# A transformer layer on one core: the first norm's scale vector spread by TensorE instead of by a broadcast load, with a renewed order table

## The chip, the cores and the metric

One core of a Trainium2 chip runs the whole layer as one program. The metric is the device time of one execution in microseconds; the time before is the median of three executions, 1282.27 us (1280.33 to 1286.3).

## The reference

One layer over x, 1024 tokens by 1024 channels, batch 1, all in f32:

```python
hn = rms_norm(x, g_mix)            # x * rsqrt(mean(x*x) + 1e-6) * g_mix
proj = hn @ w_in                   # split into 17 pieces for four token mixers
# a: compressed, selected and windowed attention with gates   b: short convolution
# c: stick-breaking attention                                 d: dilated attention
groups = rms_norm(concat(o_a, o_b, o_c, o_d), g_out)
x = x + groups @ w_out
h2 = rms_norm(x, g_ffn)
return x + (silu(h2 @ w_gate) * (h2 @ w_up)) @ w_down
```

The change touches how `g_mix`, 1024 numbers, gets to the first norm, and the order of nearly all instructions.

## The kernel before

Every f32 product is made as three TensorE products: each operand is split into a high part (a rounded copy by ACT) and a low part (the rest, by DVE or POOL), and `mm3` (L241 to L244) adds high x high, high x low and low x high into PSUM.

**The start.** TensorE gets 32 transposes of the identity matrix that nobody reads (L73 to L76, `WARM`). SP, which issues nearly all DMAs in order, loads the first 128 rows of x (512 KB, L209), the scale vector `gbc` (L212: the same 4 KB row of `g_mix` to each of the 128 partitions, 512 KB written), the next rows of x, and two tiles of weights `wr` (536 KB each, L215, the w_in columns of `wA2`). Then come small constants (L218, L429), the other x tiles, and in L132 the pieces of a further weight, `wa`.

For each of the eight x tiles `normed_rows` (L171 to L186) does: ACT squares the tile with a sum (L175), DVE scales the sum (L179), POOL raises it to the power -0.5 (L180), DVE multiplies x by that number and by `gbc` into `xn` (L185; the first tile in two halves). `norm_transpose` (L188 to L200) then has TensorE transpose `xn` in two groups of four blocks (L196) into PSUM tiles `Tp` (two buffers), from which ACT writes the high part `XH` (L199) and DVE the low part `XL` (L200). The weights in `wr` are split by ACT into `whi` (L108) and by POOL into `wlo` (L109). With those, `proj_tok` (from L255) multiplies a token tile with `wA2`, 24 matmuls of 268 columns for each tile.

**After the start** come the other projections, the attention mixers, the output product, the FFN in Strassen-like products (`winograd`, `level2`), and the last product with `w_down`.

**What sets the order.** The program is traced once. `make_plan` (L2008) plays a list scheduler over it, `_planned` (L1852): on each engine, of the instructions that are ready in its own model of durations, it takes the one with the smallest due time. `DUE` (L1359) holds the due times as differences, one for each of the 9668 instructions ahead of the last stage (`PINNED_UNTIL`); the running sum is the due time. `fix_order` (L2018) then ties each engine's instructions to the planned order. So an engine waits at an instruction of the plan even where a later one could run. The 1465 instructions of the last stage, the product with `w_down`, have no due times.

```python
        while later[e] and later[e][0][0] <= t:
            r, i = heappop(later[e])
            heappush(now[e], (due[i], i))
        i = heappop(now[e])[1]
```

Of the kernel before, what the change touches and what calls it, by code (L numbers as in the profile page):

```python
# [9 lines left out]
F32 = mybir.dt.float32  # L10
# [7 lines left out]
D = 1024  # L18
NT = T // 128
KT = D // 128  # L20
# [7 lines left out]
WARM = 32  # L28
# [24 lines left out]
def hybrid(ctx, tc, pools, x, gmix, wa1, wa2, wkv, wcv, wd, wc, bgate, gcols, pe, w1, w2,  # L53
           convw, gout, wout, gffn, wgate, wup, wdown, c_wa, c_wsp, c_wd, c_wc, c_ind, out):
    nc = tc.nc
    cst = pools(ctx, "cst")
# [12 lines left out]
    ident = identr.bitcast(F32)  # L69
# [3 lines left out]
    if WARM:  # L73
        wm = pat_.tile([128, 512], F32, tag="O", bufs=NB["O"], name="Op")
        for _ in range(WARM):
            nc.tensor.transpose(wm[:, :128], ident, ident)  # L76
    gcol = cst.tile([128, 6], F32, name="gcol")
# [129 lines left out]
    for t in range(NT):  # L207
        xt = smq.tile([128, T], F32, tag="QK", bufs=QKB, name="xt")
        nc.sync.dma_start(xt, x[t * 128:(t + 1) * 128, :])  # L209
        xts.append(xt)  # L210
        if t == 0:
            nc.sync.dma_start(gbc, bass.AP(tensor=gmix.tensor, offset=gmix.offset, ap=[[0, 128], [1, D]]))  # L212
        if t < 2:
            wr = sm.tile([128, 2 * T], F32, tag="V", bufs=2, name="wr")
            nc.sync.dma_start(wr[:, :4 * 268].rearrange("p (k n) -> p k n", n=268), wa2[:, 4 * t:4 * t + 4, :])  # L215
            wraws.append(wr)
# [240 lines left out]
    for z, src in ((0, KK), (1, VV)):  # L457
# [22 lines left out]
        tp = Ttile()  # L480
# [17 lines left out]
        if z == 0:  # L498
# [7 lines left out]
            tp = Ttile()  # L506
# [1615 lines left out]
```

## Time and profile before

| | us |
|---|---|
| median of three runs (lowest, highest) | 1282.27 (1280.33, 1286.3) |
| the profiled execution's own time | 1282.15 |
| its span in the trace | 1280.4 |
| TensorE (PE) busy | 1261.8, 99% of the span |
| weight loads (PEld) busy | 1087.2, 85% |
| VectorE (DVE) busy | 1021.0, 80% |
| ScalarE (ACT) and GpSimd (POOL) busy | 696.6 and 695.0, 54% each |

The profiled execution took 1282.15 us, 1.75 us more than its span, and lies 0.12 us below the median. An engine's busy time adds up its instructions; the remainder is idle time, which the trace puts down to what released the next instruction. All times inside the trace are counted from the start of the span.

### The profile page before, as it was taken

How to read it: one execution, taken by the hardware profiler on the slowest of the kernel's cores; microseconds unless marked ns; L12 is line 12 of the kernel's file. 1: busy time of each engine (PE TensorE's matmuls, PEld its weight loads, DVE VectorE, ACT ScalarE, POOL GpSimd, SP SyncE). 2: the span in 40 equal slices, each digit the busy share in tenths (PEclk: the TensorE clock that was granted, in tenths of full speed). 3: DMA queues.
4: the chain of work that ended last, by engine and by line, in shares of the span. 5: the costliest groups of instructions: out<-in, count | busy, mean ns of one | idle time of the engine just before them, and what ended most of it. 6: DMA issues, size and time to landing. Idle time of an engine off the chain costs nothing.

```text
span 1280.4 us, 20588 instructions
## 1 busy us (share of the span) xinstructions
PE 1261.8 (99%) x7161; PEld 1087.2 (85%) x7161; DVE 1021.0 (80%) x1843; ACT 696.6 (54%) x1383; POOL 695.0 (54%) x514
## 2 busy tenths in 40 slices
PE   8999999999999999999999999999999999999998
PEld 8888888888899898999878878888888888887887
DVE  6868888888889889844778888996888977699862
ACT  6567677768889778635653333332333335523540
POOL 6453362645557344336753556564665654665655
PEclk9999999999999999999999999999999999999999
DMA  6340030212211315544644464344324339852534
GB/s 240 110 135 1 9 108 9 75 36 54 55 38 41 91 59 173 165 132 128 221 152 138 164 204 167 124 148 147 134 100 141 120 131 336 308 181 66 148 101 155
DMA packets 91416, 161.45 MB, mean 126 GB/s; under 512 B 10224, under 2 KB 33264, under 8 KB 91312
## 3 DMA queue, kind: packets, MB, share of 16 engines
q1 hardware_dynamic: 90752, 158.31, 38.3%
q0 software_dynamic: 560, 1.84, 0.4%
q8 instruction: 56, 0.92, 0.3%
q14 instruction: 48, 0.39, 0.1%
HBM read 119.47 MB, written 36.44 MB: 122 GB/s over the span
## 4 chain that ended last, share of the span: by engine, by line
PE 91%; DVE 3%; DMA 2%; ACT 2%; issue 1%; POOL 1%; SPq 0%; DVEq 0%; POOLq 0%; ACTq 0%
PE PRp L242 12%; PE PRp L244 12%; PE PRp L243 12%; PE Tp L571 4%; PE PRp L1156 3%; PE PRp L1158 3%; PE PRp L1157 3%; PE SPp L525 2%; PE SPp L523 2%; PE Op L577 2%; PE Op L576 2%; PE Tp L1156 2%; PE Tp L1158 2%; PE Tp L1157 2%; PE SPp L1156 2%; PE SPp L1158 2%
## 5 line engine op out<-in xcount | busy, mean ns | idle before, releaser
L109 POOL TENSOR_TENSOR wlo<-raw,whi 128x512 fp32r<-128x512 f32 x94 | 128.4, 1373 | 93.5 <-ACT whi L108 64.8
L559 ACT ACTIVATE pth<-Tp 128x512 fp32r<-128x512 f32 (+2 forms) x172 | 89.4, 529 | 51.1 <-PE Tp L571 26.2
L560 DVE TENSOR_TENSOR ptl<-Tp,pth 128x512 fp32r<-128x512 f32 (+2 forms) x172 | 103.0, 605 | 16.1 <-ACT pth L559 14.5
L1227 DVE TENSOR_TENSOR fw<-sraw,fw 128x512 fp32r<-128x512 f32 x73 | 89.7, 1251 | 30.5 <-ACT fw L1226 27.7
L1145 POOL TENSOR_TENSOR fw<-fraw,fw 128x512 fp32r<-128x512 f32 x50 | 75.3, 1511 | 67.4 <-ACT fw L1144 63.4
L1227 POOL TENSOR_TENSOR hw<-bB,hw 128x512 fp32r<-128x512 f32 x55 | 82.0, 1507 | 48.5 <-ACT hw L1226 48.5
L571 PE MATMUL Tp<-ident,S 128*128 128x128 f32 x552 | 103.5, 274 | 0.6 <-DVE ptl L560 0.6
L242 PE MATMUL PRp<-XH,whi 128*128 128x512 f32 x224 | 90.6, 408 | 0.0
L244 PE MATMUL PRp<-XH,wlo 128*128 128x512 f32 x224 | 89.7, 405 | 0.0
L243 PE MATMUL PRp<-XL,whi 128*128 128x512 f32 x224 | 89.7, 406 | 0.0
L1144 ACT ACTIVATE fw<-fs 128x512 fp32r<-128x512 f32 x72 | 43.5, 628 | 84.9 <-DVE fs L1089 61.4
L654 POOL TENSOR_SCALAR S<-S,ll 128x640 f32<-128x640 f32 (+7 forms) x32 | 54.6, 1708 | 60.8 <-DVE ll L652 25.6
L108 ACT ACTIVATE whi<-raw 128x512 fp32r<-128x512 f32 x102 | 62.8, 620 | 36.6 <-PE PRp L243 21.2
L571 PEld LDWEIGHTS Tp<-ident,S 128*128 128x128 f32 x552 | 69.1, 140 | 8.8 <-DVE ptl L560 0.8
L1145 DVE TENSOR_TENSOR fw<-fs,fw 128x512 fp32r<-128x512 f32 x72 | 69.5, 985 | 3.5 <-ACT fw L1144 3.2
L804 POOL TENSOR_TENSOR S<-S,R 128x128 f32<-128x128 f32 (+7 forms) x32 | 47.7, 1491 | 42.0 <-DVE R L802 32.0
L243 PE MATMUL PRp<-wlo,MH 128*128 128x256 f32 (+1 forms) x248 | 68.7, 289 | 0.0
L242 PE MATMUL PRp<-whi,MH 128*128 128x256 f32 (+1 forms) x248 | 67.6, 291 | 0.6 <-DVE dkr L322 0.6
L244 PE MATMUL PRp<-whi,ML 128*128 128x256 f32 (+1 forms) x248 | 66.9, 288 | 0.4 <-DVE ML L831 0.4
L1226 ACT ACTIVATE hw<-bB 128x512 fp32r<-128x512 f32 x62 | 38.8, 627 | 48.3 <-PE Op L244 18.8
L1226 ACT ACTIVATE fw<-sraw 128x512 fp32r<-128x512 f32 x73 | 45.6, 625 | 28.1 <-DMA sraw<-hS 16.4
L649 ACT ACTIVATE S<-S,mm 128x640 f32<-128x640 f32 (+7 forms) x64 | 47.0, 734 | 17.9 <-DVE mm L550 15.8
(569 smaller groups left out, 4577.7 us busy)
## 6 DMA issues: line engine op xcount, KB each, us to landing
fraw<-in_wgate_dram SPq DMA_DIRECT2D x22, 512.0 KB, 4.2
fraw<-in_wup_dram SPq DMA_DIRECT2D x22, 512.0 KB, 4.3
bB<-in_wdown_dram SPq DMA_DIRECT2D x44, 256.0 KB, 5.1
sraw<-hS SPq DMA_DIRECT2D x44, 256.0 KB, 2.7
raw<-in_wout_dram SPq DMA_DIRECT2D x30, 256.0 KB, 2.9
hS<-s SPq DMA_DIRECT2D x30, 256.0 KB, 2.3
sraw<-hA SPq DMA_DIRECT2D x29, 256.0 KB, 4.0
xt<-in_x_dram SPq DMA_DIRECT2D x8, 512.0 KB, 7.4
```

What stands on the lines that cost most here:

```text
L109: (lo or nc.gpsimd).tensor_tensor(dst_lo, raw, f(dst_hi), op=OP.subtract)
L242: nc.tensor.matmul(ps, a[0], b[0], start=first, stop=False)
L243: nc.tensor.matmul(ps, a[0], b[1], start=False, stop=False)
L244: nc.tensor.matmul(ps, a[1], b[0], start=False, stop=last)
L559: nc.scalar.activation(ph[:, c], tp[:, :n], AF.Copy)
L560: nc.vector.tensor_tensor(pl[:, c], tp[:, :n], f(ph[:, c]), op=OP.subtract)
L571: nc.tensor.transpose(tp[:, i * 128:(i + 1) * 128], p, ident)
L1145: eng.tensor_tensor(wt[:, 1, :], a, f(wt[:, 0, :]), op=OP.subtract)
L1156: nc.tensor.matmul(ps, wt[:, 0, c], bh[:, k, :], start=k == 0, stop=False)
L1158: nc.tensor.matmul(ps, wt[:, 1, c], bh[:, k, :], start=False, stop=k == 3)
L1226: nc.scalar.activation(wt[:, 0, :], raw, AF.Copy)
L1227: eng.tensor_tensor(wt[:, 1, :], raw, f(wt[:, 0, :]), op=OP.subtract)
```

## The change

Three things. `g_mix` comes from the host as 8 columns of 128 and is loaded as that, 4 KB in pieces of 32 bytes for each partition (`gmc`). Eight TensorE transposes of a column repeated 128 times put it into two `Tp` tiles, every partition with the same row, and two DVE copies bring them to `gbc`. The warm-up transposes go from 32 to 20. And the `DUE` list is another one over its whole length (9666 entries), fitted to the new program.

```diff
-WARM = 32
+WARM = 20
...
         for _ in range(WARM):
             nc.tensor.transpose(wm[:, :128], ident, ident)
+    gmc = cst.tile([128, KT], F32, name="gmc")
+    nc.sync.dma_start(gmc, gmix)
...
         if t == 0:
-            nc.sync.dma_start(gbc, bass.AP(tensor=gmix.tensor, offset=gmix.offset, ap=[[0, 128], [1, D]]))
+            for j in range(2):
+                tp = Ttile()
+                for k in range(4):
+                    nc.tensor.transpose(tp[:, k * 128:(k + 1) * 128],
+                                        gmc[:, 4 * j + k:4 * j + k + 1].to_broadcast([128, 128]), ident)
+                nc.vector.tensor_copy(gbc[:, j * 512:(j + 1) * 512], tp)
...
 DUE = """
--37755 1210 -1715 1864 149 -14756 334 80 152 75 -251 117 106 28 150 49 116 89 66 141 46 40 143 102 107 12 67 74 -27
...
-    d["gmix"] = np.asarray(i["g_mix"])[0]
+    d["gmix"] = np.asarray(i["g_mix"])[0].reshape(8, 128).T
```

The running sums of the two lists for what stands at the start of SP and TensorE (a smaller one goes first among those that are ready):

| instruction | due before | due after |
|---|---|---|
| DMA `gbc` (512 KB) / `gmc` (4 KB) | -38254 | -29488 |
| DMA x tile 0 | -37893 | -29435 |
| DMA `wr`, first half | -37152 | -28452 |
| DMA `wa`, first piece (256 KB) | -36029 | -28237 |
| DMA `go` (4 KB) | -36860 | -27871 |
| DMA `wr`, second half | -37815 | -27812 |
| DMA `pet` (16 KB) | -34613 | -25747 |
| DMA x tile 1 | -37588 | -25173 |
| DMA x tile 5 | -36383 | -25067 |
| DMA x tile 2 | -37062 | -24551 |
| first five warm-up transposes | -51003 to -50362 | -42099 to -41823 |
| the other 27 / 15 warm-up transposes | -50613 to -48756 | -38185 to -37391 |
| eight transposes of `gmc` | none | -42495 to -38644 |

SP follows these sums at the start but for `wr`, whose tiles come behind x tile 1 before the change. In the attention part (100 to 550 us of the planner's own time) the sums before and after differ by some hundreds and are correlated by 0.9 and more in each 50 us. In the first 100 us and from 600 us on (the FFN) they differ by thousands and up, with a correlation below 0.9, in some 50 us of the FFN near zero.

## Rows read from the trace of the kernel before

**Rows 1.** The page's first part: busy us of each engine (share of the span), instructions.
```profile
PE 1261.8 (99%) x7161; PEld 1087.2 (85%) x7161; DVE 1021.0 (80%) x1843; ACT 696.6 (54%) x1383; POOL 695.0 (54%) x514
```

**Rows 2.** Windows: start:end, length, busy us (instructions) of PE..POOL, granted clock, DMA share, GB/s.
```profile
40.00:120.00 80.00, 77.15 (x542) 70.85 (x541) 59.97 (x166) 49.72 (x130) 38.21 (x33) 1.00 0.26 82
760.00:800.00 40.00, 38.38 (x190) 30.97 (x189) 34.28 (x50) 13.72 (x26) 25.32 (x18) 1.00 0.52 178
800.00:1060.00 260.00, 260.00 (x1240) 215.09 (x1239) 222.32 (x278) 90.26 (x163) 155.68 (x109) 1.00 0.39 132
1080.00:1120.00 40.00, 40.00 (x173) 32.21 (x172) 25.82 (x21) 23.38 (x42) 26.58 (x18) 1.00 0.91 316
```

**Rows 3.** Timeline: start, us, engine, line, what, xcount [idle before <- releaser]. Warm-ups, x0.
```profile
2.21 6.66 PE L76 MATMUL Op<-ident 128*128 128x128 f32 x32 [2.21 <-DVE ident L72]
...
4.44 1.06 ACT L175 ACTIVATE xn<-xt 128x1024 f32<-128x1024 f32 x1 [2.43 <-DMA xt<-in_x_dram]
...
5.62 0.15 DVE L179 TENSOR_SCALAR ssm<-ss 128x1 f32<-128x1 f32 x1 [3.46 <-ACT xn L175]
...
6.53 1.42 DVE L185 SCALAR_TENSOR_TENSOR xn<-xt,ss,gbc 128x512 f32<-128x512 f32 x2 [0.76 <-POOL ss L180]
...
8.71 1.04 PE L196 MATMUL Tp<-ident,xn 128*128 128x128 f32 x8
```

**Rows 4.** Timeline: x tile 1, the weight split, the first matmuls.
```profile
7.83 1.06 ACT L175 ACTIVATE xn<-xt 128x1024 f32<-128x1024 f32 x1 [2.24 <-DMA xt<-in_x_dram]
...
9.57 0.60 ACT L199 ACTIVATE XH<-Tp 128x512 fp32r<-128x512 f32 x1 [0.59 <-PE Tp L196]
9.83 1.29 DVE L185 SCALAR_TENSOR_TENSOR xn<-xt,ss,gbc 128x1024 f32<-128x1024 f32 x1 [0.67 <-POOL ss L180]
10.06 0.64 ACT L108 ACTIVATE whi<-wr 128x536 fp32r<-128x536 f32 x1
...
10.75 0.39 PE L242 MATMUL PRp<-whi,XH 128*128 128x268 f32 x1 [1.01 <-ACT whi L108]
10.78 2.82 POOL L109 TENSOR_TENSOR wlo<-wr,whi 128x536 fp32r<-128x536 f32 x2 [0.98 <-ACT whi L108]
11.04 1.28 DVE L200 TENSOR_TENSOR XL<-Tp,XH 128x512 fp32r<-128x512 f32 x2
...
11.78 0.65 PE L196 MATMUL Tp<-ident,xn 128*128 128x128 f32 x4 [0.63 <-DVE XL L200]
...
12.36 0.40 PE L243 MATMUL PRp<-wlo,XH 128*128 128x268 f32 x1
...
12.71 0.28 PE L242 MATMUL PRp<-whi,XH 128*128 128x268 f32 x1
...
12.84 0.28 PE L243 MATMUL PRp<-wlo,XH 128*128 128x268 f32 x1
```

**Rows 5.** Windows at the start (columns as in Rows 2).
```profile
0.00:4.44 4.44, 2.23 (x11) 2.23 (x12) 0.73 (x7) 1.29 (x2) 1.29 (x11) 1.00 0.55 172
0.00:7.83 7.83, 5.62 (x27) 5.62 (x28) 2.19 (x10) 2.44 (x4) 1.85 (x12) 1.00 0.73 248
...
7.00:8.00 1.00, 1.00 (x6) 1.00 (x5) 0.94 (x2) 0.17 (x1) 0.00 (x0) 1.00 0.99 385
8.00:9.00 1.00, 1.00 (x10) 1.00 (x9) 0.00 (x0) 0.98 (x2) 0.00 (x0) 1.00 1.02 412
```

**Rows 6.** Timeline of SP: the first issue.
```profile
0.73 0.39 SPq L209 DMA_DIRECT2D xt<-in_x_dram  x1
```

**Rows 7.** DMA issues: what, queue, count, KB each, median us from issue to landing.
```profile
go<-in_gout_dram SPq DMA_DIRECT2D x1, 4.0 KB, 8.4
zq<-cqh SPq DMA_DIRECT2D x16, 32.0 KB, 1.8
```

**Rows 8.** Window from the end of the last matmul (columns as in Rows 2).
```profile
1276.66:1280.40 3.74, 0.00 (x0) 0.00 (x0) 0.69 (x1) 0.00 (x0) 0.00 (x0) 1.00 0.37 140
```

**Rows 9.** A window of the last stage (columns as in Rows 2).
```profile
1175.00:1185.00 10.00, 8.44 (x29) 6.18 (x28) 10.00 (x9) 4.91 (x9) 8.31 (x5) 0.83 0.25 63
```

638 rows, old and new, of the table DUE are left out of this document.

## The prediction

> **What bounds the kernel now.** I read the busy times first: TensorE is busy for 1261.8 of the span's 1280.4 us [rows 1], so all its idle time is 18.6 us. Then wide windows, to see whether busy means full pace: in 1080 to 1120 us, 173 matmuls take 40.00 us, 0.231 us each, and from 800 to 1060 us TensorE does not idle at all [rows 2]. Then the timeline of the start, because that is what the change rebuilds.
>
> There the reader is to see this. TensorE runs 32 warm-up transposes from 2.21 us on, 6.66 us long. x tile 0 has landed by 4.44 us, its scale is there just before 6.53, and DVE makes `xn` in two halves of 0.71 us each; the first is ready at 7.24. Yet its transposes begin at 8.71, behind the last warm-up [rows 3]. Then TensorE idles for 1.01 us until `whi` is there (10.75) and for 0.63 us until a `Tp` buffer is free (11.78), and has continuous work from 12.36 on [rows 4]. Meanwhile the loads run at 385 to 412 GB/s [rows 5]. x tile 1 lands at 7.83, behind `gbc`.
>
> TensorE bounds the kernel, so a saving counts only where it takes idle time out of TensorE or lets its real work start sooner. At the start that is 1.64 us of idle time and what the warm-ups hold back.
>
> [...]
>
> **The warm-ups and the spread.** Removed: 12 transposes of the identity. Added: 8 of `gmc`. The 32 cost 6.66 us, 0.208 each, so 28 end at 2.21 + 28 x 0.208 = 8.03 instead of 8.7. By the due sums the eight stand behind the first few warm-ups, with 15 behind them. `gmc` is issued first, so x tile 0 goes one issue later, about 0.4 us [rows 6]; its first half of `xn` is then ready at 7.24 + 0.4 = 7.65, covered by the warm-ups. The two copies to `gbc` are new on DVE; the nearest row is `XL`, 0.64 us each [rows 4]. They fall where DVE idles, 3.46 us ahead of L179 [rows 3], and end by about 6, before the scale of tile 0 (6.4 + 0.4). So x0's transposes start at about 8.15 instead of 8.71: **0.55 us** sooner.
>
> When does `gmc` land? No row has a 4 KB load into empty queues. The nearest are 1.8 us for 32 KB in a quiet part and 8.4 us for the 4 KB of `go` behind 2 MB of loads [rows 7]. It is first, so I take 2 us: 0.73 + 2 = 2.7 us, after two or three warm-ups, no wait. At 8.4 it would be 9.1 us, and TensorE, whose order is fixed, would stand at the first transpose of `gmc` with 15 warm-ups and all of x0 queued behind it (the last rival).
>
> The pace: six transposes start in the us before 8.0 and ten in the next [rows 5], the same instruction at 0.208 us and then at about half of that. [...] Afterwards 28 transposes stand there, and I take the rise where it was. If it comes later, x0's eight transposes take 1.7 instead of about 0.9 us and the first matmuls double too: up to 1.3 us lost. If it comes earlier, next to nothing is gained.
>
> [...]
>
> **The load taken out, and the new order of loads.** There are 512 KB less to move, 1.3 us at 400 GB/s. But the due sums also put weights first: x0, `wr`, a piece of `wa`, `go`, `wr`, `pet`, and only then x1. When x1 landed, 7.83 x 248 = 1942 KB had moved, 400 KB more than the three loads up to it hold; for x0 it was 4.44 x 172 = 764 KB, 250 KB more [rows 5]. With 330 to 400 KB:
> - `wr`, first half: 1052 + 330 KB, moved at about 6.4 us. `whi` (0.64) can follow then instead of at 10.06, and two `wlo` (POOL, 1.41 each [rows 4]) by 10. The wait for `whi` goes.
> - x1: 2376 + 330 to 400 KB, moved at 9.7 to 9.9 instead of 7.83: **2 us later**.
>
> What is late next: from x0's transposes to its `XH` it is 9.57 - 8.71 = 0.86 us, and 0.60 for ACT, so the first matmul goes from 10.75 to about 8.15 + 1.51 = 9.66. x0's 24 matmuls at 0.125 (two starts, 12.71 and 12.84) take 3.0 us, until 12.7. x1 needs 11.12 - 7.83 = 3.29 us from landing to `xn` [rows 4], so it is there at 13.1. TensorE idles 0.4 us for it and 0.6 us for its `XH`, until 14.7. By then it has done 0.87 + 3.0 + 0.87 = 4.74 us of real work (a group of eight transposes counted as 0.87). Before, by 14.7, it had done 0.87 for x0, 0.56 (four transposes and one matmul) and 14.7 - 12.36 = 2.34: 3.77. **Ahead by 0.97 us**, which contains the 0.55. From there on both run without gaps, as an x tile comes every 1.3 us and feeds 3.9 us. Bounds: all idle time gone and the earlier start, 1.64 + 0.55 = 2.2 us gained; or x1 later still and the rise missed, 1 us lost.
>
> **The due times of the rest.** No row shows what a new order costs. Idle time left to win: 18.6 less 2.2 ahead of the first instruction, 1.6 at the start and 3.7 behind the last matmul [rows 8] is 11 us, of which 2.85 lie in 40 to 120 us and 1.6 in 760 to 800 [rows 2]. To lose: a stall such as the one at 1175 to 1185, where TensorE idles for 1.56 us and the granted clock falls to its lower level for a while, 0.83 as a mean of 10 us [rows 9]: 1.7 us more, 3.3 in all. (That stall lies in the last stage, which has no due times.) I take a gain of 0.9 us, a third of the 2.85, because the loads of the next projections' weights move ahead most there; the bounds are a gain of 7.8 us (third rival) and a loss of 6.6 (two such stalls).
>
> **Sum.** 1282.15 (the profiled execution, 0.12 below the median) - 0.97 - 0.9 = 1280.3 us. A measurement of this kernel can tell about 0.5%, 6.4 us, from no change: faster is below 1275.9, slower above 1288.7. So I forecast no change that can be told, a shade on the fast side: chance 0.56, with 1278 to 1283 as its own range.
>
> **Rivals.**
> - *The start is given back* (0.12). x1's 2 us of delay, or a later wait for an x tile, takes what the earlier weights bring. For it: x1 has the longest chain at the start. Against: x0 alone feeds 3 us. Time: 1282.2.
> - *The new order stalls TensorE in the FFN* (0.15), the case on the slow side. Place: 800 to 1060 us, where it never idles, so nothing can be won. Price: 1.6 us for a stall (as in 760 to 800, clock at 1.00), 3.3 with the clock's fall. One such stall decides against the gains, two with the fall give 1280.3 + 6.6 = 1286.9, three 1290.2. For it: the due sums there hardly resemble the old ones. Against: 260 us without one now.
> - *The new order tightens TensorE* (0.14). The stall in 760 to 800 (1.6), the 2.85 us in 40 to 120 and the 3.3 at 1175 go: 1282.15 - 0.97 - 7.8 = 1273.4; half of it 1277.3. For it: the first 100 us are reordered most. Against: the attention part keeps nearly its old order.
> - *`gmc` lands late* (0.03). At 9.1 us TensorE still has 23 transposes, 4.8 us, ahead of x0's: 13.9 instead of 8.71, less the 1.64 us of idle time, +3.5: 1285.6. It decides from about 3.3 us on, when the first five warm-ups are done.
>
> **How the numbers follow.** Below 1275 lies about half of the third rival and a tail, 0.09; above 1287 half of the second and a tail, 0.10: the range is 1275 to 1287. Faster: most of the third rival and a tail of the forecast, 0.15. Slower: three stalls, or two and a lost start, 0.08. Same: 0.77.
>
> **What would show it.** Right: x0's transposes (L196) at 8.1 to 8.2 us; the wait for `whi` gone; x1's square (L175) at about 9.8; the first matmul at about 9.7; TensorE 0.5 to 1.5 us ahead when x tile 1 is through. Wrong at the pace: x0's transposes 0.2 us apart. Wrong at `gmc`: TensorE idle among the warm-ups. Wrong in the rest: TensorE idle between 800 and 1060 us, or a granted clock below 1.00 there. What would overturn the forecast is an idle sum in the middle that has moved from 11 us by more than 5.

## The result, and the profile after

The changed kernel takes 1273.46 us (median of five runs, 1271.28 to 1274.95), the kernel before 1282.27 (five runs by now, 1280.33 to 1286.3), 8.8 us more. The ratio is 0.9927 [0.9913, 0.9941], 0.73% faster, more than the 0.5% that can be told from no change. I had forecast 1280.3, in a range of 1275 to 1287. The profiled execution took 1274.13 us.

The page of the changed kernel, span and busy times (beside [rows 1]):

```profile
span 1272.4 us, 20600 instructions
PE 1249.0 (98%) x7157; PEld 1085.9 (85%) x7157; DVE 1012.7 (80%) x1845; ACT 696.4 (55%) x1383; POOL 700.7 (55%) x514
```

TensorE's idle time did not shrink: 1272.4 - 1249.0 = 23.4 us, 4.8 more than before. Its busy time shrank, by 12.8 us, with four matmuls fewer. So I cut each span just ahead of the first matmul of the FFN (at 672.8 before, at 675.5 after; columns as in [rows 2]). Before:

```profile
0.00:672.80 672.80, 661.11 (x4436) 598.08 (x4437) 529.01 (x1255) 475.52 (x991) 344.69 (x273) 1.00 0.31 97
672.80:1280.40 607.60, 600.67 (x2727) 489.11 (x2725) 492.02 (x589) 221.08 (x393) 350.31 (x241) 1.00 0.48 158
```

After:

```profile
0.00:675.50 675.50, 661.74 (x4432) 598.50 (x4433) 523.04 (x1256) 474.50 (x990) 350.51 (x273) 0.99 0.31 96
675.50:1272.40 596.90, 587.31 (x2727) 487.36 (x2725) 489.62 (x590) 221.85 (x394) 350.24 (x241) 1.00 0.48 161
```

Three numbers carry the result. Ahead of the FFN the changed kernel's profiled execution is 2.7 us **behind** (executions with the old start differ by as much, see below). In the FFN and the last stage the same 2727 matmuls keep TensorE busy for 13.4 us less, at the same granted clock. And TensorE idles there for 9.6 us instead of 6.9, so 10.7 of the 13.4 us arrive. No instruction of the FFN was changed. What did change in it is seen in the groups by line and form (busy us, mean ns of one), in 800 to 1060 us. Before:

```profile
L1156 PE MATMUL PRp<-T,fw 128*128 128x512 f32 x73 | 28.5, 395 | 0.0
```

After:

```profile
L1163 PE MATMUL PRp<-T,fw 128*128 128x512 f32 x74 | 28.9, 390 | 0.0
```

The matmul of 512 columns is 5 ns shorter here. Since these matmuls overlap (395 ns of one before, and the next starts some 233 ns after it), the distance from one start to the next is the better measure. Its mean over successive 512-column matmuls, without the distances above 300 ns, which hold a wait, is 233.2 ns in the FFN and 233.3 ns in the last stage before, 227.6 and 226.9 ns after. Some 2,270 of them by 5.9 ns are 13.4 us. Ahead of the FFN the same distance is 233 ns in both kernels.

The last stage shows it without any wait, in the window of 1080 to 1120 us after the change (columns as in [rows 2], whose last row is the same window before, with 173 matmuls):

```profile
1080.00:1120.00 40.00, 40.00 (x178) 33.14 (x177) 27.30 (x25) 22.64 (x41) 27.04 (x18) 1.00 0.87 301
```

The start, where I had looked for the gain, went backwards. Timeline of the changed kernel (columns as in [rows 3], with which it is to be compared):

```profile
2.11 1.54 PE L76 MATMUL Op<-ident 128*128 128x128 f32 x6 [2.11 <-DVE ident L72]
...
3.45 1.78 PE L217 MATMUL Tp<-ident,gmc 128*128 128x128 f32 x8
...
4.54 1.42 DVE L219 COPY gbc<-Tp 128x512 f32<-128x512 f32 x2 [2.49 <-PE Tp L217]
...
4.96 1.06 ACT L177 ACTIVATE xn<-xt 128x1024 f32<-128x1024 f32 x1 [2.95 <-DMA xt<-in_x_dram]
5.07 1.69 PE L76 MATMUL Op<-ident 128*128 128x128 f32 x14
...
6.31 1.19 ACT L110 ACTIVATE whi<-wr 128x536 fp32r<-128x536 f32 x2 [0.20 <-DMA wr<-in_wa_dram]
...
6.98 2.47 DVE L187 SCALAR_TENSOR_TENSOR xn<-xt,ss,gbc 128x512 f32<-128x512 f32 x2 [0.69 <-POOL ss L182]
7.04 4.88 POOL L111 TENSOR_TENSOR wlo<-wr,whi 128x536 fp32r<-128x536 f32 x3
...
9.60 1.06 PE L198 MATMUL Tp<-ident,xn 128*128 128x128 f32 x8 [2.84 <-DVE xn L187]
...
11.29 1.06 ACT L177 ACTIVATE xn<-xt 128x1024 f32<-128x1024 f32 x1 [1.09 <-DMA xt<-in_x_dram]
...
12.35 0.58 ACT L201 ACTIVATE XH<-Tp 128x512 fp32r<-128x512 f32 x1
...
12.98 0.59 PE L249 MATMUL PRp<-whi,XH 128*128 128x268 f32 x1 [2.32 <-ACT XH L201]
```

The weights come early, as forecast (`whi` at 6.31). But POOL's `wlo` now runs beside DVE's `xn` (from 7.04 us on), whose two halves take 2.47 us instead of 1.42 [rows 3]. The runs below show the same: in e4, where `wlo` starts 0.06 us after the first half as it does here, the two take 2.47 us; in e7 x tile 1's `xn`, begun 0.06 us after `wlo`, takes 2.33 us instead of the 1.29 of [rows 4], where it begins 0.95 us ahead of `wlo`; in e11, where `wlo` starts at 8.91, behind both halves, these take 1.41 us. Why it is slower there was not looked into.

And x tile 1 lands at 11.29. ACT's order has its square ahead of the `XH` of tile 0, which waits behind it until 12.35. So TensorE idles 2.8 and 2.3 us, and then runs at about half rate for a while: from 14.1 to 16.1 us its matmuls of 268 columns start 0.22 us apart, from 18.7 us on 0.12 to 0.13. The window (columns as in [rows 2]) reads a granted clock of 0.50:

```profile
14.00:16.00 2.00, 2.00 (x10) 2.00 (x10) 1.51 (x3) 0.99 (x2) 0.93 (x1) 0.50 1.04 398
```

### The profile page after: what moved, and what is told of

Read it like the earlier page. It is cut to its first block, busy times and chain, and to the rows that moved or that the text cites. A ratio compares the mean times of both kernels' runs of the same rounds, so it can differ in the third digit from the quotient of the medians.

```text
span 1272.4 us, 20600 instructions
## 1 busy us (share of the span) xinstructions
PE 1249.0 (98%) x7157; PEld 1085.9 (85%) x7157; DVE 1012.7 (80%) x1845; ACT 696.4 (55%) x1383; POOL 700.7 (55%) x514
## 4 chain that ended last, share of the span: by engine, by line
PE 87%; DVE 7%; DMA 2%; issue 2%; POOL 1%; ACT 0%; SPq 0%; DVEq 0%; POOLq 0%; ACTq 0%
PE PRp L249 12%; PE PRp L251 12%; PE PRp L250 12%; PE Tp L578 4%; PE PRp L1165 3%; PE PRp L1163 3%; PE PRp L1164 3%; PE SPp L530 2%; PE Op L584 2%; PE SPp L532 2%; PE Op L583 2%; PE SPp L1165 2%; PE SPp L1163 2%; PE Tp L1165 2%; PE SPp L1164 2%
## 5 line engine op out<-in xcount | busy, mean ns | idle before, releaser
L111 POOL TENSOR_TENSOR wlo<-raw,whi 128x512 fp32r<-128x512 f32 x94 | 131.8, 1407 | 97.9 <-ACT whi L110 74.5
L1234 POOL TENSOR_TENSOR hw<-bB,hw 128x512 fp32r<-128x512 f32 x55 | 82.3, 1512 | 45.5 <-ACT hw L1233 45.4
L1152 DVE TENSOR_TENSOR fw<-fs,fw 128x512 fp32r<-128x512 f32 x72 | 63.8, 904 | 2.7 <-ACT fw L1151 2.4
L249 PE MATMUL PRp<-whi,XH 128*128 128x256 f32 (+1 forms) x192 | 55.1, 294 | 2.9 <-ACT XH L201 2.3
```

The costliest lines, as they stand in the source:

```text
L111: (lo or nc.gpsimd).tensor_tensor(dst_lo, raw, f(dst_hi), op=OP.subtract)
L249: nc.tensor.matmul(ps, a[0], b[0], start=first, stop=False)
L1152: eng.tensor_tensor(wt[:, 1, :], a, f(wt[:, 0, :]), op=OP.subtract)
L1234: eng.tensor_tensor(wt[:, 1, :], raw, f(wt[:, 0, :]), op=OP.subtract)
```

## The experiments

**The theories.** One thing in the change touches the FFN besides the order: `gmc`. It is 32 bytes for each partition in the constants' pool, on the left side of SBUF, and every tile allocated behind it on that side moves up by 32 bytes. The weights of the FFN (`fw`, stationary) lie on the right side and stay. So the first theory (A) is that the gain is one of **placement** of the moving operand against the stationary one. The rival is the renewed order of the FFN. A third theory (C) concerns the loss at the start: it comes from x tile 1's load, and would go if that load were issued before the spread. In the kernels below, "left" and "right" are unused tiles that shift one side by their size.

**1. e1: the shift alone.** The kernel before, with nothing but an unused tile of 32 bytes:

```diff
+    cst.tile([128, 8], F32, name="pad")
```

> The kernel before, with its own order and its own start, and one unused tile of 32 bytes per partition in the constants' pool, so that every left-hand tile (X, T, B, the last stage's hw) lies 32 bytes higher, as gmc makes it in the changed kernel. Theory A (the FFN's gain is the relative place of the two operands: left-hand moving operand and right-hand weights fw either both at 0 or both at 32 modulo 64 bytes): the 512-column matmuls of the FFN start 0.227 us apart instead of 0.233, about 2,240 of them save 6.5 ns each, 14.5 us, and the start stays as before, so 1267 to 1269 us. Theory B (the renewed due times bring the gain): no change, 1282.

Measured: 1273.55 us (1271.58 to 1274.0), ratio 0.9931 [0.9916, 0.9946]; the distance in the FFN is 227 ns. An unused tile, with the old load and the old due times, brings what the change brings. It is less than the 13 to 15 us expected: TensorE's busy time from the FFN on is 586.1 us, 14.6 less than before, but its idle time there is 10.3 us instead of 6.9, and this profiled execution is 3.0 us behind at the FFN's first matmul, with the old start.

**2. e2: the changed kernel, shifted once more.**

```diff
+    cst.tile([128, 8], F32, name="pad")
     gmc = cst.tile([128, KT], F32, name="gmc")
```

> The changed kernel with the same 32 unused bytes beside gmc, so that left-hand tiles lie 64 bytes above where they were before, back at 0 modulo 64. Theory A: 0.233 us between the FFN's matmuls again, 1273.5 + 14 = 1286 to 1288 us, slower than before the change by the start's loss. Theory B: 1273.

Measured: 1283.25 us (1281.6 to 1285.01), ratio 1.0005 [0.9996, 1.0014]. The group of the same line, in 800 to 1060 us of e2:

```profile
L1164 PE MATMUL PRp<-T,fw 128*128 128x512 f32 x74 | 29.2, 395 | 0.0
```

All of the gain is gone, with the new load, the new order and the new start in place: what the change does by intention is worth nothing that can be told. I had expected 1286 to 1288 us, for a loss at the start that this time does not show.

**3. e3: the kernel before, the right side shifted.**

```diff
+    pools(ctx, "padr", side="right").tile([128, 8], F32, name="padr")
     smq = pools(ctx, ...)
```

> The kernel before with an unused tile of 32 bytes on the right-hand side instead, so that the weights fw lie at 0 modulo 64 like the unmoved left-hand tiles. Theory A (equal remainders of the two operands): 0.227 us, 1267 to 1269 us. Theory A2 (the moving operand itself has to lie at 32 modulo 64): 0.233 us, 1282. Theory B: 1282.

Measured: 1270.92 us (1270.34 to 1271.71), ratio 0.9915 [0.9899, 0.9932], distance 227 ns. Moving the right side down does the same as moving the left side up: it is the distance between the two that counts.

**4. e4: the changed start with the old due times**, mapped instruction by instruction; the new instructions get due times near those of what they replace.

```diff
 DUE = """
--28774 18 69 71 1396 -14879 69 43 79 85
+-37755 1210 -1715 1864 149 -14756 334 80 152 75
...
```

> The changed kernel (gmc, its eight transposes, 20 warm-ups, left-hand tiles at 32 modulo 64) with the due times of before for all instructions that both have. Theory A: the FFN at 0.227 us, and the start without the weights-first order of loads; x tile 1 lands before 7.8 us, TensorE does not idle 2.8 and 2.3 us as in the changed kernel, so 1266 to 1269 us. Theory B: the gain is gone, 1281 to 1283.

Measured: 1275.51 us (1272.95 to 1277.71), ratio 0.9949 [0.9929, 0.9968]: about the change's time, without its order, and 6 to 9 us above what theory A had it at. The start is little better: the first matmul stands at 11.45 instead of 12.98, but `xn` is as slow, and TensorE waits for it as long:

```profile
7.30 2.47 DVE L187 SCALAR_TENSOR_TENSOR xn<-xt,ss,gbc 128x512 f32<-128x512 f32 x2 [0.68 <-POOL ss L182]
...
9.92 1.06 PE L198 MATMUL Tp<-ident,xn 128*128 128x128 f32 x8 [2.96 <-DVE xn L187]
...
11.45 0.39 PE L249 MATMUL PRp<-whi,XH 128*128 128x268 f32 x1 [0.47 <-ACT XH L201]
```

**5. e5: the renewed order alone.** e1, with the changed kernel's due times for all that is planned after 100 us (a mapped `DUE` list, as in e4).

> The kernel before with the 32 bytes on the left (as e1), its own start, and the renewed due times for every instruction that the old plan starts after 100 us; the old ones before that. If the renewed order is worth something behind the start (the changed kernel is 2.0 us behind e1 at its 1200th matmul and level with it at the end): 1271 to 1272 us. If its order is worth nothing there and the lead came from what the start left over: 1273.5 as e1.

Measured: 1273.59 us (1272.61 to 1274.77), ratio 0.9928 [0.9913, 0.9944], the time of e1 to within 0.04 us. The renewed order of the rest is worth nothing that can be seen.

**6. e6: does placement count ahead of the FFN too?** e1 with the split weights 544 instead of 536 words apart:

```diff
-    WS = 536
+    WS = 544
-        return main.tile([128, WS], F32R, tag="whl", bufs=WHB, name=name)
+        return main.tile([128, WS], F32R, tag="whl", bufs=WHB, name=name)[:, :536]
```

> e1 with the pitch of the split weights (whl and raw tiles) 544 instead of 536 columns, so that all of them, X and fw lie at 32 modulo 64. In e1 only half of the weight tiles match X. If the equal remainder helps the 512-column matmuls ahead of the FFN too: about 560 of them at 0.227 instead of 0.232, 2.8 us less than e1, 1270.7. If their pace is set by something else (other operand shapes between them): 1273.5 as e1.

Measured: 1271.85 us (1269.51 to 1272.95), ratio 0.9913 [0.9897, 0.9929]. The distance ahead of the FFN stays at 233 ns, so this pitch is not what sets it there. The interval overlaps that of e1. It is no test of the rule found in part 9: by e6's own allocation half of these weight tiles start at a distance of 0 modulo 256 bytes from the moving operand's pool and half at 128. Whether placement counts ahead of the FFN stays open.

**7. e7 and e11: the spread behind x tile 1's load.** In the code `gbc` and the x tiles take their places from one ring, in order of first use. `gbc` is now first used by the copies, ahead of x tile 1, so the planner can place x1's load only behind the copies, with the new due times and with the old ones (e4). In the kernel before the same ring put x tile 0's load ahead of that of `gbc`, against their due times. One line moves the spread, and x1's due time is put ahead of those of the weights (e7 is built on e4, e11 on the changed kernel):

```diff
         xts.append(xt)
-        if t == 0:
+        if t == 1:
             for j in range(2):
                 tp = Ttile()
```

> e4 (gmc, old due times) with the block that spreads gmc written behind the load of x tile 1 instead of ahead of it, so that in the ring of 1024-column tiles x1 comes before gbc and its load goes second, ahead of the weights. Theory C (the start lost because x1 stood behind the weights in the ring's order and because wlo on POOL then runs beside xn on DVE): xn's two halves take 1.4 us in all instead of 2.47, x1 has landed by 6.6 to 7 us, the first matmul comes at about 10, and the time is 2 to 3 us below e4, 1272.5 to 1273.5. Theory D (the start lost through the clock alone, which falls at about 12 us in e1, e3 and e4 alike): as e4, 1275.5.

Measured for e7: 1272.68 us (1270.45 to 1274.57), ratio 0.992 [0.9903, 0.9936], 2.8 us below e4, though the two intervals overlap.

> The changed kernel, renewed due times and all, with the block that spreads gmc written behind the load of x tile 1, so that x1's load goes second and ACT no longer stands before x1's square with x0's high part queued behind it. Theory C (x1 behind the weights is the start's loss): TensorE's first 50 matmuls take 10 to 11 us instead of 14.4, and 3.5 us are gained, 1270. If the start's loss is made up further on anyway: 1273.

Measured for e11: 1270.78 us (1269.13 to 1271.97), ratio 0.9902 [0.9888, 0.9916], 2.7 us below the changed kernel: the lowest time of all runs, though its interval touches that of the change. Its timeline:

```profile
6.10 1.06 ACT L177 ACTIVATE xn<-xt 128x1024 f32<-128x1024 f32 x1
...
6.83 1.41 DVE L187 SCALAR_TENSOR_TENSOR xn<-xt,ss,gbc 128x512 f32<-128x512 f32 x2 [0.68 <-POOL ss L182]
...
8.39 1.06 PE L198 MATMUL Tp<-ident,xn 128*128 128x128 f32 x8 [0.46 <-ACT whi L110]
...
9.93 0.39 PE L249 MATMUL PRp<-whi,XH 128*128 128x268 f32 x1 [0.47 <-ACT XH L201]
```

x tile 1's square runs at 6.10 instead of 11.29, `xn` takes 1.41 us again, and the first matmul stands at 9.93 instead of 12.98. The first matmul of the FFN comes at 673.8 us instead of 675.6. So the waits at the start shrank with x1's place, as theory C says. The time is less sure: the intervals overlap or touch, and theory D is not excluded, since in the profiles of e7 and e11 the clock does not seem to fall at 12 us either: the granted clock of e11 is 1.00 over the first 40 us, and e7's matmuls of 268 columns start 0.12 to 0.13 us apart from 13.8 to 14.4 us, against 0.22 at a clock of 0.50 in the changed kernel (e4 reads 0.52 and 0.62 in 12 to 16 us, by 2 us).

**8. e8: right shift with the new order** (e5 with the tile of e3 instead of that of e1), to see whether e3's lead over e1 repeats:

```diff
+    pools(ctx, "padr", side="right").tile([128, 8], F32, name="padr")
-    cst.tile([128, 8], F32, name="pad")
```

> e5's order with the pad on the right instead of the left (as e3): both operands at 0 modulo 64. If e3's lead over e1 (1270.9 to 1273.55) is a matter of where the tiles lie: 2 to 3 us below e5. If it is chance of the runs or of the stalls of that order: as e5.

Measured: 1271.38 us (1270.68 to 1273.87), ratio 0.9914 [0.9896, 0.9931]. The lead of 2.2 to 2.6 us repeats, at the same 227 ns. In the profiles of e1 and e3 the FFN begins at 675.8 and 673.8 us, so 2.0 of the 3.5 us between their spans lie ahead of it; the intervals overlap, and the cause stays open.

**9. Which distance is fast?** Six kernels narrow the rule down, and theory A in its narrow form (equal remainders of 64 bytes are fast) falls to theory E (the distance counts modulo 256 bytes, fast at 0).

e9, 96 bytes on the left of the kernel before:

```diff
+    cst.tile([128, 24], F32, name="pad")
```

> The kernel before with 96 unused bytes on the left instead of 32 (e1): left-hand tiles and fw then have the same remainder modulo 64 bytes (32) and different ones modulo 128 (32 against 96). If 64 bytes is what counts: 0.227 us between the FFN's matmuls, about 1273 as e1. If it is 128 bytes: 0.233, 1282.

Measured: 1274.74 us (1274.69 to 1275.82), ratio 0.9937 [0.9924, 0.995]. The distance is 229 ns, between the two that were expected.

e10 and e12, e7 and e11 with 96 bytes on the left and 32 on the right, so that both operands start at a multiple of 64 bytes:

```diff
+    pools(ctx, "padr", side="right").tile([128, 8], F32, name="padr")
+    cst.tile([128, 24], F32, name="pad")
```

> e7 with the left-hand tiles 96 bytes further up and the right-hand ones 32 down, so that both operands of the FFN lie at 0 modulo 64 instead of both at 32. If 0 is better than 32 by itself (e3 is 2.6 us below e1, e8 2.2 below e5): 1270 to 1270.5. If those two pairs differ by chance: 1272.7 as e7.

> e11 with both operands at 0 modulo 64, as e10: the candidate that should beat both kernels. With theory C and 0 better than 32: 1268. With theory C alone: 1270. With neither: 1273.

Measured: 1279.99 us (1276.94 to 1283.22), ratio 0.9974 [0.9962, 0.9987], and 1280.18 us (1278.32 to 1285.07), ratio 0.9979 [0.9968, 0.9989], some 7 to 9 us above e7 and e11, at 233 ns in the FFN. The narrow form of A is wrong.

e13 and e14, 288 and 160 bytes on the left of the kernel before, where E says fast and slow:

```diff
+    cst.tile([128, 72], F32, name="pad")
```

> The kernel before with 288 unused bytes on the left. Theory E (what counts is the distance from the left-hand tiles to the right-hand ones modulo 256 bytes; fast at 0: after, e1, e3 and e11 at 0 with 0.227 us, e9 at 192 with 0.229, e10 at 128 with 0.2326, before and e2 at 32 and 224 with 0.233): the distance is 168,448 bytes, 0 modulo 256, so 0.227 us and about 1272. Theory A (equal remainders modulo 64, with something else in e10 and e12): 0.227 as well. Theory F (the distance of 168,704 bytes itself, or a larger period): 0.229 to 0.233, 1275 to 1282.

```diff
+    cst.tile([128, 40], F32, name="pad")
```

> The kernel before with 160 unused bytes on the left: the distance is e10's, 168,576 bytes (128 modulo 256), with the start and the due times of before. Theory E: 0.2326 us, 1279 to 1281. Theory A, in which e10's and e12's pace comes from something else in these kernels (both pads, gmc's start): equal remainders modulo 64, so 0.227, 1272.

Measured: 1272.39 us (1271.35 to 1275.06), ratio 0.9928 [0.9906, 0.9951], and 1280.37 us (1278.67 to 1282.14), ratio 0.9981 [0.9968, 0.9994]. Both came as E said. The last stage in 1080 to 1120 us, first e13, then e14 (columns as in [rows 2], whose last row is the same window of the kernel before):

```profile
1080.00:1120.00 40.00, 40.00 (x178) 33.15 (x177) 28.80 (x25) 22.50 (x41) 27.80 (x19) 1.00 0.87 299
```

```profile
1080.00:1120.00 40.00, 40.00 (x173) 32.20 (x172) 25.16 (x24) 22.85 (x41) 25.33 (x18) 1.00 0.89 310
```

178 matmuls in 40 us against 173, TensorE busy throughout in both, at a granted clock of 1.00.

e16, 224 bytes on the left, to see whether it is as good to be 64 bytes off on this side as on that of e9:

```diff
+    cst.tile([128, 56], F32, name="pad")
```

> The kernel before with 224 unused bytes on the left: a distance of 168,512 bytes, 64 modulo 256, the other side of e9's 192. Theory E with a cost that grows with how far the distance is from 0: about 0.229 us, 1274 to 1276. If only e9's side is cheap: 0.232 or more, 1280. Theory A: 0.227, 1272.

Measured: 1281.83 us (1278.39 to 1284.11), ratio 0.9996 [0.9984, 1.0009], at 233 ns. It is not, and a cost that grows with how far the distance is from 0 is wrong as well.

**10. e15: the last stage alone.** The kernel before, with 32 bytes ahead of the last stage's own tiles only:

```diff
     f2 = pools(ctx, "f2", ...)
+    f2.tile([128, 8], F32, name="pad")
```

> The kernel before with 32 unused bytes ahead of the last stage's tiles alone, so that only its moving operand hw is 32 bytes higher; X, T and B stay. If the place of the moving operand sets the pace of the matmuls that read it: 0.233 us in the FFN up to 1,060 us as before, 0.227 in the last stage, whose 924 matmuls save 5.6 us less what stalls take: 1277 to 1278. If the pace is set by where other left-hand tiles lie: no change, 1282.

Measured: 1278.66 us (1275.76 to 1281.32), ratio 0.9974 [0.9963, 0.9985]. Groups by line and form, one of the FFN (800 to 1060 us) and one of the last stage (1080 to 1120 us):

```profile
L1156 PE MATMUL PRp<-T,fw 128*128 128x512 f32 x74 | 28.9, 396 | 0.0
...
L243 PE MATMUL SPp<-hw,fw 128*128 128x512 f32 x22 | 8.6, 389 | 0.0
```

In the kernel before, the second group reads:

```profile
L243 PE MATMUL SPp<-hw,fw 128*128 128x512 f32 x22 | 8.7, 396 | 0.0
```

Within one program the shifted stage is fast and the other is not; the last stage alone brings 1281.95 - 1278.66 = 3.3 us of the 9.6 that e13 brings on the same chip. The shift moves all left-hand tiles of this stage; that the moving operand is the one that counts is inferred, as it is the only one of them that TensorE reads.

**All of it in one table.** D is the distance from the start of the moving operand's pool on the left to that of the stationary operand's ring on the right, in bytes, by the kernel's own allocation. The distance between starts is in ns, the mean without those above 300 ns, in the FFN and in the last stage.

| kernel | D | D mod 256 | ns, FFN / last stage |
|---|---|---|---|
| before | 168,736 | 32 | 233.2 / 233.3 |
| after, e1, e3 to e8, e11 | 168,704 | 0 | 227.5 to 227.7 / 226.7 to 226.9 |
| e2 | 168,672 | 224 | 233.1 / 233.3 |
| e9 | 168,640 | 192 | 229.2 / 228.9 |
| e10, e12, e14 | 168,576 | 128 | 232.3 to 232.7 / 232.8 to 232.9 |
| e16 | 168,512 | 64 | 233.2 / 233.3 |
| e13 | 168,448 | 0 | 227.5 / 226.8 |
| e15, FFN / last stage | 168,736 / 168,704 | 32 / 0 | 233.2 / 226.8 |

Remainder 0 was tried at two distances, 256 bytes apart, and the others at one distance each, so the period of 256 bytes rests on those two. What in the chip makes it so was not looked into, and distances that are no multiple of 32 bytes were not tried.

## Why the prediction was wrong

**The reading of the bound failed.** The step was "a saving counts only where it takes idle time out of TensorE or lets its real work start sooner". I took 173 matmuls in 40 us for full pace, because TensorE was busy and its clock was full [rows 2], and concluded that the FFN had nothing to win. The same window holds 178 after the change: the saving lies in the pace of the busy time, 13.4 us of it. With no idle time and a granted clock of 1.00, TensorE worked 3% below the pace that it had after the change (173 matmuls against 178), and neither the matmul's share (40.00 us of 40 in both) nor that of the weight loads (32.21 and 33.14 of 40 us) says so plainly. Over the whole span the share of weight loads did not show the gain either: it was 85% before and after. As to my test for being overturned, an idle sum in the middle that moves from 11 us by more than 5: from 40 us to the last matmul TensorE idled for 10.7 us before and for 12.3 after. The test did not trip, and the forecast was wrong all the same, so it was the wrong sum to watch.

**The sum left out where things lie.** Its parts were loads, transposes, copies, warm-ups and due times. It had no term for the 32 bytes that `gmc` takes. They are the only part of the change with an effect on the time that the runs can tell (e1 against e2).

**The start: -0.97 us forecast, no gain found.** Point by point:

- Right: `gmc` early, its transposes at 3.45 without a wait; copies of 0.71 us, off the path; x tile 0 half a microsecond later (4.96); `whi` at 6.31 for a forecast of 6.4, and the wait for it gone.
- Wrong, the start of x0's transposes: 9.60 for 8.15. I had them held by the warm-ups until 8.03, and ready after the first half of `xn`. The warm-ups were done at 5.07 + 1.69 = 6.76 and held nothing. x0's transposes begin behind the second half in each run looked at: 6.98 + 2.47 = 9.45, then 9.60; in e11 6.83 + 1.41 = 8.24, then 8.39. And I missed that the earlier weights put POOL's `wlo` beside `xn`: 1.05 us more.
- Wrong, x tile 1: landed at 11.29 for 9.8. Its load stood behind the weights, as forecast from the due sums; that the ring would put it there even with the old ones (e4) I had not seen. Why it came 1.5 us later still was not looked into. I had a delay, but not that ACT's square of x1 stands ahead of x0's `XH` and passes the delay on to work that was ready.
- Wrong, the first matmul: 12.98 for 9.66. The half-rate stretch behind that I had not priced at all. It can't be laid to the change alone, as e1's profile has one too, with the old start: over the first 40 us the granted clock is 1.00 in the profile before, 0.96 in e1 and 0.91 after the change, and the first 50 matmuls of 268 columns take 9.1, 11.0 and 10.7 us. (My sum there also has a slip: its terms end at 14.6 us, not 14.7, which is worth 0.1 us.)

In the profiles of before and after this is 2.7 us at the FFN's first matmul, but that much is no measure of the change. e15 is the kernel before in all that lies ahead of the last stage, and its profiled execution reaches the FFN at 675.1 us; the kernels with the old start and an unused tile reach it at 673.1 to 676.8. One difference between such executions is the clock: in 12 to 16 us it reads 1.00 in the profile of before, and 0.61 and 0.54, by 2 us, in that of e1. In the medians e2, whose pace in the FFN is that of before, is at 1.0005 [0.9996, 1.0014]: no gain, and a loss that can't be told from none. e7 and e11 come 2.8 and 2.7 us below e4 and the changed kernel by one moved line and x1's due time, about as much as e3 lies below e1 for no known cause.

**The renewed due times: -0.9 us forecast.** TensorE's idle time in 40 to 120 us, where I had looked for it, went from 2.85 to 2.10 us in the profile, but in the time e5 shows nothing. Between 800 and 1060 us TensorE idled for 0.43 us, so the second rival's mechanism was not seen.

**The third rival** gave 1273.4 us, which is the time that came. It was right by accident: its stalls did not go. Of the 2.85 us in 40 to 120 us 2.10 stayed, the 1.6 in 760 to 800 became 1.8, and the stall at 1175 [rows 9] became two, though the clock no longer fell there. Waits of TensorE after the change (us in total, times, longest):

```profile
PE Tp L198 <- DVE xn L187: 2.8, 1, 2.8
PE PRp L249 <- ACT XH L201: 2.3, 1, 2.3
PE Tp L250 <- POOL hw L1234: 2.2, 2, 1.1
```

The first two are the start. The third is the last stage, where POOL's `hw` arrives late twice by 1.1 us, once before. The window of 1160 to 1200 us holds both (columns as in [rows 2]):

```profile
1160.00:1200.00 40.00, 36.80 (x157) 29.05 (x156) 37.00 (x38) 20.50 (x37) 27.87 (x18) 1.00 0.39 112
```

TensorE idles for 3.2 us there, 1.6 more than the 1.56 of [rows 9]. e1, with the old order, has the same two waits, so I put them down to the higher pace, at which TensorE meets suppliers that kept theirs (the 55 `hw<-bB,hw` of POOL in the last stage have a mean of 1507 ns before and 1512 after). This is most of the 2.7 us by which the 13.4 came short.

## What to carry to other kernels

A small tile added to a kernel moves everything behind it; before a gain or a loss is put down to the edit, run the old kernel with an unused tile of that size, and the new one with another. Read TensorE's pace from the time between the starts of one form of matmul, and compare it between stages and kernels: here a busy share of 100% in a window of 40 us hid 3%. And when a load is made cheap, look at what its tile's slot and the freed loads let in: here x tile 1 came later (11.29 us instead of 7.83), and with the weights earlier `xn` ran beside `wlo` and took 2.47 us instead of 1.42.

## What the runs showed of the hardware

In the FFN and the last stage the distance between the places of moving and stationary operand sets the pace of the f32 matmul of 512 columns with a weight load for each. By the distance modulo 256 bytes it is 226.7 to 227.7 ns at 0, 229 at 192, 232.3 to 232.9 at 128, and 233.1 to 233.3 at 32, 64 and 224. Between the ends that is 2.5% in the FFN and 2.9% in the last stage. That it is the place and not the order or the start is seen in e1 (an unused tile alone, 227 ns and 1273.55 us), e2 (the change with such a tile, 233.1 ns and 1283.25 us) and e15 (both paces in one program, 233.2 and 226.8 ns).

As in [rows 5], the transposes' pace rose with nothing but transposes before it: the changed kernel's first six warm-ups end 1.54 us after they begin, 0.26 each, its last fourteen take 1.69, 0.12 each. When the rise comes differs between executions: the same 32 warm-ups take 6.66 us in [rows 3] and 5.35 in e1.

```profile
2.21 5.35 PE L76 MATMUL Op<-ident 128*128 128x128 f32 x32 [2.21 <-DVE ident L72]
```
